# Two small masks of the linear mixers on ScalarE and GpSimd instead of VectorE, and twelve matmuls without a reader

## The chip, the cores and the metric

The kernel runs on one core of a Trainium2 chip. The engines of a core each work through a queue of their own, in order: PE (TensorE, matmuls), DVE (VectorE), ACT (ScalarE), POOL (GpSimd) and SP (which here issues the loads of weights). An instruction waits at the head of its queue until the semaphores say that what it reads is written and what it overwrites has been read. The metric is the device time of one execution, in microseconds (us), as the median of several runs. Of PE the profile also gives the granted clock: 1.00 is 2.4 GHz, 0.50 is 1.2 GHz.

## The reference

For 256 tokens of width 1024 a network of four layers is computed, all in fp32. Two layers of the first kind come first, f0 and f1:

```python
for l in range(DEPTH):                       # DEPTH = 2
    h = rms_norm(x, pre_mix_g[l])
    z = h @ w_in[l]                          # split into the inputs of four mixers
    o_a = hgrn2_mixer(a_q, a_f, a_i, a_g, ...)       # chunk_gla, 64 wide keys
    o_b = gla_mixer(b_q, b_k, b_v, b_code, b_g, ...) # chunk_gla, 32 wide keys
    o_c = mla_mixer(...)                             # softmax attention
    o_d = gdn_mixer(...)                             # gated delta rule
    mix = jnp.concatenate([o_a, o_b, o_c, o_d], axis=-1) @ w_out[l]
    x = x + rms_norm(mix, post_mix_g[l])
    h = rms_norm(x, pre_ffn_g[l])
    y = conv_glu_ffn(h, w_gate[l], w_up[l], conv_w[l], w_down[l])
    x = x + rms_norm(y, post_ffn_g[l])
```

Mixers a and b, which the change is about, share one form. Within a chunk of 64 tokens it is

```python
diff = b_[:, :, :, None, :] - b_[:, :, None, :, :]     # b_: running sum of log gates, per key channel
decay = jnp.where(causal, jnp.exp(jnp.where(causal, diff, 0.0)), 0.0)
attn = jnp.einsum('bhid,bhjd,bhijd->bhij', q_, k_, decay)
o = einsum(attn, v_) + einsum(q_ * exp(b_), state)
```

so each entry of `attn` needs a decay of its own for each channel, and only entries with j <= i count. Two layers of a second kind (s0, s1: four softmax attentions, a wide FFN, a gated embedding) follow.

## The kernel before

**Matmuls.** The weights come in fp32 by DMAs that SP issues, into tiles `raw`. ACT copies `raw` to a rounded high half `wh` (L300), and DVE, for some units POOL, subtracts to get the low half `wl` (L303). A product is three matmuls, high by high, high by low, low by high (`mm3`, L329 to L331). The tokens are two tiles of 128, t = 0 and 1; in the projections that close a layer, `acc` are the PSUM banks of tile 0 and `pc` those of tile 1.

**A layer of the first kind.** `norms` with `steps` (L454 to L514) makes the normed input: squares summed by ACT (L428) and DVE (L437), a power on POOL (L241), the product `nxn` on DVE (L502), eight transposes on PE (L505), and the halves by ACT (L510) and DVE (L512). The stretch from the last matmuls of one part through these steps to the first matmuls of the next I call a boundary; here its kind is 'in' where it leads into f1, '2in' where it leads into s0 or s1. Then the four mixers run in phases, in the order d, b, a, c with their first and second parts interleaved. I call the stretch with d's preparation and the body of b stage 1 (82 to 98 us in f0, 466 to 496 us in f1), and the one with the body of a, the attention of c and the end of d stage 2 (130 to 199 us, 515 to 592 us). Stage 2 ends in the output projection, `big_out`, whose units are taken in the order d, c, a, b.

**The body of a and b, `gla` (L691).** `A[t]`, 128 tokens by 4 heads by 128 tokens, collects `attn`, transposed, for tile t. For the diagonal, PE multiplies k by q (L704) and DVE multiplies the result by the identity (L705), which also zeroes the rest of `A[t]`. The rest goes level by level: at level s each block of 2s tokens gives its lower left square of s by s, in which the decays can be split at the middle of the block, so that one exponential each for rows and columns is enough. Gates are differenced on DVE and POOL (L721 to L728), exponentiated on ACT (L729), multiplied into q by DVE (`gl_r`, L733) and into k by POOL (`gl_e`, L737); PE multiplies (L743, L751). Level 128 goes to its own tile X, level 64 is copied by ACT (L756), levels 32, 16, 8, 4, 2 and 1 by DVE with a mask (L760), two instructions each. Then PE multiplies `A[t]` and X by v (L768, L769), and `head_norm` (L597) closes: square on ACT (L601), sum on DVE (L603), power on POOL (L236, L241), two products on DVE (`hn_y` L606, `hn_o` L608), transposes on PE (L415), halves `mT` by ACT (L417) and DVE (L418). The gla bodies of both mixers write the PSUM banks `pa`, two buffers in turn; `gla` is called four times.

**What sets the order.** Within mixers a scheduler that simulates a timeline orders each engine's queue as the program is built. At the boundaries the orders of PE or DVE are written out by hand. `warm` (L444) issues matmuls that nobody reads; `WARM` says how many for which tile.

Of the kernel before, what the change touches and what calls it, by code (L numbers as in the profile page):

```python
# [16 lines left out]
AF = mybir.ActivationFunctionType  # L17
OP = mybir.AluOpType
# [15 lines left out]
PEORD = ('in', '2in')  # L34
# [9 lines left out]
ASPL = 1  # L44
NEAR = 6
GATE = {"in": (3, 6), "ffn": (3, 4), "2in": (3, 4), "2ffn": (3, 4), "ple": (3, 4), "end": (3, 4)}
WARM = ((0, 0, 0), (0, 2, 0))

def steps_in_order(text):
    return [("AB".index(o[0]), int(o[1:])) for o in text.split()]  # L50
# [89 lines left out]
class K:  # L140
# [282 lines left out]
    def sum_sq(self, a, b, psum=False):  # L423

        nc = self.nc
        ssq = self.s(2, "ssq")
        sc = self.z([128, 512], "nsc", dt=BF)
        nc.scalar.activation(sc, a, AF.Square, scale=1.0 / 32, accum_out=ssq[:, 0:1])  # L428
        self.warm(sc, WARM[self.g == "a"][0 if psum else 2])
        yield  # L430
        if psum:
            sc = self.z([128, 512], "nsc", dt=BF)
            nc.scalar.activation(sc, b, AF.Square, scale=1.0 / 32, accum_out=ssq[:, 1:2])
            self.warm(sc, WARM[self.g == "a"][1])
        else:
            sc = self.z([128, 512], "nsc")
            nc.vector.scalar_tensor_tensor(sc, b, 1.0 / D, b, op0=OP.mult, op1=OP.mult, accum_out=ssq[:, 1:2])  # L437
        yield
        m = self.s(1, "msq")
        nc.vector.tensor_scalar(m, ssq[:, 1:2], ssq[:, 0:1], EPS, op0=OP.add, op1=OP.add)  # L440
        self.r = self.pow(m, 1)
        yield
# [248 lines left out]
    def gla(self, nft, b, qm, k, v, finish, g):  # L691

        nc = self.nc
        n = nft * 256
        ft = [0, 1] if nft == 2 else [0, 0]
        A = [self.z([128, 4, 128], "gl_a") for _ in range(2)]
        for t in range(2):  # L700
            ts = slice(t * 128, t * 128 + 128)
            p = self.pt().rearrange("p (h i) -> p h i", h=4)
            for j in range(2):
                nc.tensor.matmul(p[:, 2 * j:2 * j + 2], k[:, ft[j], ts], qm[j][:, :, ts], start=True, stop=True)  # L704
            nc.vector.tensor_tensor(A[t], p, self.ident[:, None, :].to_broadcast([128, 4, 128]), OP.mult)  # L705
            yield
        b4 = b.rearrange("p f (c s) -> p f c s", s=64)
        last = [b4[:, :, c, 63:64].to_broadcast([128, nft, 64]) for c in range(4)]
        for lv, s in enumerate((128, 64) + LEVELS):
            E = self.z([128, nft, 256], "gl_e", g)  # L710
            ev = E.rearrange("p f (b two s) -> p f b two s", two=2, s=s)
            e4 = E.rearrange("p f (c s) -> p f c s", s=64)
            if s == 128:
                nc.vector.tensor_tensor(e4[:, :, 1], last[1], b4[:, :, 1], OP.subtract)
                nc.vector.tensor_tensor(e4[:, :, 0], last[0], b4[:, :, 0], OP.subtract)
                nc.vector.tensor_tensor(e4[:, :, 0], e4[:, :, 0], last[1], OP.add)
                nc.gpsimd.tensor_copy(e4[:, :, 2], b4[:, :, 2])
                nc.vector.tensor_tensor(e4[:, :, 3], b4[:, :, 3], last[2], OP.add)
            elif s == 64:
                for c in (0, 2):  # L720
                    nc.vector.tensor_tensor(e4[:, :, c], last[c], b4[:, :, c], OP.subtract)  # L721
                    nc.gpsimd.tensor_copy(e4[:, :, c + 1], b4[:, :, c + 1])
            else:
                bv = b.rearrange("p f (b two s) -> p (f b) two s", two=2, s=s)
                ee = E.rearrange("p f (b two s) -> p (f b) two s", two=2, s=s)
                ref = bv[:, :, 0, s - 1:s].to_broadcast([128, n // (2 * s), s])
                nc.vector.tensor_tensor(ee[:, :, 1], bv[:, :, 1], ref, OP.subtract)
                nc.gpsimd.tensor_tensor(ee[:, :, 0], ref, bv[:, :, 0], OP.subtract)  # L728
            nc.scalar.activation(E, E, AF.Exp)  # L729
            R = self.z([128, 2, 2, 128], "gl_r", g)  # L730
            for j in range(2):
                qv = qm[j].rearrange("p h (b two s) -> p h b two s", two=2, s=s)[:, :, :, 1]
                nc.vector.tensor_tensor(R[:, j].rearrange("p h (b s) -> p h b s", s=s),  # L733
                                        ev[:, ft[j], :, 1][:, None].to_broadcast([128, 2, 128 // s, s]), qv, OP.mult)
            kv = k.rearrange("p f (b two s) -> p (f b) two s", two=2, s=s)
            kk = E.rearrange("p f (b two s) -> p (f b) two s", two=2, s=s)
            nc.gpsimd.tensor_tensor(kk[:, :, 0], kk[:, :, 0], kv[:, :, 0], OP.mult)  # L737
            yield
            p = self.pt()
            if s == 128:  # L740
                p = p.rearrange("p (j h i) -> p j h i", j=2, h=2)
                for j in range(2):
                    nc.tensor.matmul(p[:, j], E[:, ft[j], :128], R[:, j], start=True, stop=True)  # L743
                X = self.z([128, 4, 128], "gl_x")
                nc.scalar.activation(X, p.rearrange("p j h i -> p (j h) i"), AF.Copy)
                continue
            M = 64 if s == 64 else 128
            p = p[:M].rearrange("p (t j h i) -> p t j h i", t=2, j=2, h=2)
            for t in range(2):
                for j in range(2):  # L750
                    nc.tensor.matmul(p[:, t, j], E[:, ft[j], t * 128:t * 128 + M], R[:, j, :, t * 64:t * 64 + 64],  # L751
                                     start=True, stop=True)
            for t in range(2):
                pv = p[:, t].rearrange("p j h i -> p (j h) i")
                if s == 64:
                    nc.scalar.activation(A[t][:64, :, 64:128], pv, AF.Copy)  # L756
                    continue
                nb = 64 // s
                mask = self.cu[:, (lv - 2) * 64:(lv - 1) * 64].rearrange("p (b s) -> p b s", s=s)
                nc.vector.copy_predicated(A[t].rearrange("p h (b two s) -> p h b two s", two=2, s=s)[:, :, :, 1],  # L760
                                          mask[:, None].to_broadcast([128, 4, nb, s]),
                                          pv.rearrange("p h (b s) -> p h b s", s=s))
        yield
        for t in range(2):
            o = self.pt()[:, :256].rearrange("p (h d) -> p h d", h=4)
            for h in range(4):
                if t:
                    nc.tensor.matmul(o[:, h], X[:, h], v(0)[:, h * 64:h * 64 + 64], start=True, stop=False)  # L768
                nc.tensor.matmul(o[:, h], A[t][:, h], v(t)[:, h * 64:h * 64 + 64], start=not t, stop=True)  # L769
            finish(t, o)  # L770
            yield
# [1016 lines left out]
```

## Time and profile before

| what | value |
|---|---|
| median of 3 runs | 1531.16 us (1528.4 to 1532.23) |
| the profiled execution | 1537.6 us |
| its span, first to last instruction | 1535.9 us |
| mean granted clock of PE | 0.989 |
| PE busy | 1481.3 us, 96% |
| DVE busy | 1062.3 us, 69% |
| ACT busy | 837.2 us, 55% |
| POOL busy | 281.8 us, 18% |

Busy shares are averages over stages with different limits: DVE with 69% over the span is busy without a break in some stretches of the mixers. So what one engine's instruction is worth has to be read from the stage that it stands in. A busy PE at clock 0.50 takes twice as long for the same matmul.

### The profile page before, as it was taken

To read this page: it belongs to the slowest core of one execution; us is meant where nothing else is said; L and a number is where in the kernel's file an instruction comes from. 1 tells how busy PE (TensorE), PEld (TensorE's weight loads), DVE (VectorE), ACT (ScalarE), POOL (GpSimd) and SP (SyncE) were. 2 spreads that over 40 slices of the span, in tenths; PEclk is the share of its full clock that TensorE was granted. 3 is DMA by queue.
4 is the path that set the end of the run, shared out by engine and by line. 5 is a ranking of instruction groups with operands and counts; after the bars stand their busy time and mean duration, and the time that the engine had idled before them with its cause. 6 is when DMAs were issued, how large, how long until landed. Compare 5 with 4: busy or idle time off the path is not lost.

```text
span 1535.9 us, 23550 instructions
## 1 busy us (share of the span) xinstructions
PE 1481.3 (96%) x8731; PEld 1287.0 (84%) x8739; DVE 1062.3 (69%) x1891; ACT 837.2 (55%) x1520; POOL 281.8 (18%) x375
## 2 busy tenths in 40 slices
PE   7999999999998999999999999999998999999998
PEld 7988888888897987888978887888877888888886
DVE  6897577667789756777766866566657695666655
ACT  5735456556574534655545665544554675544453
POOL 1544210000254322000042122000024231100010
PEclk9999999999999999999999999999999999999999
DMA  7422146666452214666646334566653533465663
GB/s 238 150 84 100 52 140 184 190 190 213 135 161 78 93 42 134 183 192 187 206 131 184 110 112 124 187 191 191 211 186 111 163 121 108 133 192 187 190 202 108
DMA packets 156418, 233.99 MB, mean 152 GB/s; under 512 B 11700, under 2 KB 118158, under 8 KB 156302
## 3 DMA queue, kind: packets, MB, share of 16 engines
q1 hardware_dynamic: 156302, 232.48, 49.0%
q8 instruction: 69, 1.13, 0.3%
q14 instruction: 47, 0.39, 0.1%
HBM read 231.40 MB, written 1.05 MB: 151 GB/s over the span
## 4 chain that ended last, share of the span: by engine, by line
PE 79%; DVE 10%; ACT 4%; POOL 2%; DMA 2%; issue 2%; SPq 0%; ACTq 0%; DVEq 0%; POOLq 0%
PE pa L375 8%; PE pd L375 7%; PE acc L329 7%; PE acc L331 7%; PE acc L330 7%; PE pc L329 5%; PE pc L331 5%; PE pc L330 5%; PE pd L376 4%; PE pa L376 4%; PE pa L329 2%; PE pa L331 2%; PE pa L330 2%; DVE wl L303 2%; DVE gl_r L733 1%
## 5 line engine op out<-in xcount | busy, mean ns | idle before, releaser
L303 DVE TENSOR_TENSOR wl<-raw,wh 128x1024 fp32r<-128x1024 f32 (+4 forms) x424 | 487.1, 1157 | 310.2 <-ACT wh L300 308.6
L300 ACT ACTIVATE wh<-raw 128x1024 fp32r<-128x1024 f32 (+4 forms) x420 | 433.1, 1035 | 368.9 <-PE pc L331 92.1
L303 POOL TENSOR_TENSOR wl<-raw,wh 128x1024 fp32r<-128x1024 f32 (+1 forms) x26 | 61.2, 2358 | 641.8 <-ACT wh L300 611.2
L375 PE MATMUL pa<-xT,wh 128*128 128x512 f32 x392 | 145.9, 397 | 0.0
L375 PE MATMUL pd<-xT,wh 128*128 128x512 f32 x392 | 145.7, 397 | 0.0
L376 PE MATMUL pd<-xT,wl 128*128 128x256 f32 x392 | 110.2, 281 | 0.3 <-DVE wl L303 0.3
L376 PE MATMUL pa<-xT,wl 128*128 128x256 f32 x392 | 110.1, 281 | 0.0
L375 PEld LDWEIGHTS pd<-xT,wh 128*128 128x128 f32 x392 | 73.6, 188 | 16.8
L375 PEld LDWEIGHTS pa<-xT,wh 128*128 128x128 f32 x392 | 73.7, 188 | 12.3
L330 PE MATMUL acc<-wl,f_h 128*128 128x512 f32 x200 | 78.0, 390 | 0.0
L330 PE MATMUL pc<-wl,f_h 128*128 128x512 f32 x200 | 77.8, 389 | 0.0
L331 PE MATMUL pc<-wh,f_l 128*128 128x512 f32 x200 | 77.5, 389 | 0.0
L331 PE MATMUL acc<-wh,f_l 128*128 128x512 f32 x200 | 77.3, 391 | 0.0
L376 PEld LDWEIGHTS pd<-xT,wl 128*128 128x128 f32 x392 | 74.0, 189 | 3.6 <-DVE wl L303 0.5
L376 PEld LDWEIGHTS pa<-xT,wl 128*128 128x128 f32 x392 | 74.1, 189 | 3.6
L330 PE MATMUL acc<-wl,xT 128*128 128x512 f32 (+4 forms) x200 | 71.1, 357 | 1.6 <-DVE wl L303 1.6
L329 PE MATMUL acc<-wh,xT 128*128 128x512 f32 (+4 forms) x200 | 71.5, 361 | 1.2 <-ACT xT L510 0.8
L329 PE MATMUL pc<-wh,f_h 128*128 128x512 f32 x200 | 71.4, 390 | 0.0
L331 PE MATMUL acc<-wh,xT 128*128 128x512 f32 (+4 forms) x200 | 70.4, 354 | 0.6 <-DVE xT L512 0.6
L329 PE MATMUL acc<-wh,f_h 128*128 128x512 f32 x200 | 67.0, 391 | 0.0
L329 PE MATMUL acc<-wh,mT 128*128 128x512 f32 (+2 forms) x136 | 51.4, 387 | 1.6 <-ACT mT L510 1.4
L330 PE MATMUL acc<-wl,mT 128*128 128x512 f32 (+2 forms) x136 | 51.3, 378 | 0.0
(651 smaller groups left out, 3852.5 us busy)
## 6 DMA issues: line engine op xcount, KB each, us to landing
raw<-in_w_in_dram SPq DMA_DIRECT2D x84, 512.0 KB, 4.2
raw<-in_w_mlp_up_dram SPq DMA_DIRECT2D x64, 512.0 KB, 3.7
raw<-in_w_mlp_down_dram SPq DMA_DIRECT2D x64, 512.0 KB, 3.6
raw<-in_ffn_w_gate_dram SPq DMA_DIRECT2D x44, 512.0 KB, 3.6
raw<-in_ffn_w_up_dram SPq DMA_DIRECT2D x44, 512.0 KB, 3.9
raw<-in_ffn_w_down_dram SPq DMA_DIRECT2D x44, 512.0 KB, 3.6
raw<-in_w_out_dram SPq DMA_DIRECT2D x32, 512.0 KB, 3.6
raw<-in_w_ple_gate_dram SPq DMA_DIRECT2D x16, 512.0 KB, 4.4
```

The costliest lines, as they stand in the source:

```text
L300: nc.scalar.activation(h[:, p], raw[:, p], AF.Copy)
L303: e.tensor_tensor(l[:, p], raw[:, p], h[:, p].bitcast(F), OP.subtract)
L329: t.matmul(out, ah, bh, start=first, stop=False, skip_group_check=True)
L330: t.matmul(out, ah, bl, start=False, stop=False, skip_group_check=True)
L331: t.matmul(out, al, bh, start=False, stop=last, skip_group_check=True)
L375: t.matmul(out[f], h[:, k, c], xT.both[:, :, kk], start=kk == 0, stop=False, skip_group_check=True)
L376: t.matmul(out[f][:, 1], l[:, k, c], xT[0][:, kk], start=False, stop=kk == 7, skip_group_check=True)
L733: nc.vector.tensor_tensor(R[:, j].rearrange("p h (b s) -> p h b s", s=s), ev[:, ft[j], :, 1][:, None].to_broadcast([128, 2, 128 // s, s]), ...
```

## The change

Three edits. (1) At the boundaries of kinds 'in' and '2in', tile 0's sum of squares before the mixers (`sum_sq` without PSUM) is followed by four matmuls of the identity by the square `nsc`, 512 columns each, that nobody reads. There are three such boundaries: f0 to f1 (at 391 us), f1 to s0 (784) and s0 to s1 (1157). (2) The diagonal of `A[t]`: instead of the product with the identity on DVE, ACT copies the PSUM bank to `A[t]`, and POOL sets to zero what lies on one side of the diagonal; the levels overwrite the entries on the other side. (3) Level 32 is copied by ACT, four copies of 32 rows in each call of `gla`, two for each tile, without a mask.

```diff
--- before.py
+++ after.py
@@ -44,7 +44,7 @@
 ASPL = 1
 NEAR = 6
 GATE = {"in": (3, 6), "ffn": (3, 4), "2in": (3, 4), "2ffn": (3, 4), "ple": (3, 4), "end": (3, 4)}
-WARM = ((0, 0, 0), (0, 2, 0))
+WARM = ((0, 0, 0, 4), (0, 2, 0, 0))
 
 def steps_in_order(text):
     return [("AB".index(o[0]), int(o[1:])) for o in text.split()]
@@ -426,7 +426,7 @@
         ssq = self.s(2, "ssq")
         sc = self.z([128, 512], "nsc", dt=BF)
         nc.scalar.activation(sc, a, AF.Square, scale=1.0 / 32, accum_out=ssq[:, 0:1])
-        self.warm(sc, WARM[self.g == "a"][0 if psum else 2])
+        self.warm(sc, WARM[self.g == "a"][0 if psum else 2 + (self.near > 0 and self.kinds[self.near] in PEORD)])
         yield
         if psum:
             sc = self.z([128, 512], "nsc", dt=BF)
@@ -702,7 +702,10 @@
             p = self.pt().rearrange("p (h i) -> p h i", h=4)
             for j in range(2):
                 nc.tensor.matmul(p[:, 2 * j:2 * j + 2], k[:, ft[j], ts], qm[j][:, :, ts], start=True, stop=True)
-            nc.vector.tensor_tensor(A[t], p, self.ident[:, None, :].to_broadcast([128, 4, 128]), OP.mult)
+
+            nc.scalar.activation(A[t], p, AF.Copy)
+            nc.gpsimd.affine_select(out=A[t], in_=A[t], pattern=[[0, 4], [1, 128]], compare_op=OP.is_ge, fill=0.0,
+                                    base=0, channel_multiplier=-1)
             yield
         b4 = b.rearrange("p f (c s) -> p f c s", s=64)
         last = [b4[:, :, c, 63:64].to_broadcast([128, nft, 64]) for c in range(4)]
@@ -754,6 +757,10 @@
                 pv = p[:, t].rearrange("p j h i -> p (j h) i")
                 if s == 64:
                     nc.scalar.activation(A[t][:64, :, 64:128], pv, AF.Copy)
+                    continue
+                if s == 32:
+                    for r in (0, 64):
+                        nc.scalar.activation(A[t][r:r + 32, :, r + 32:r + 64], pv[r:r + 32, :, r // 2:r // 2 + 32], AF.Copy)
                     continue
                 nb = 64 // s
                 mask = self.cu[:, (lv - 2) * 64:(lv - 1) * 64].rearrange("p (b s) -> p b s", s=s)
```

In the linear mixers of both layers the schedule is laid out anew by the scheduler, with the same result in f0 and f1 in stage 2. Three places follow, in the rows of the engines' queues; line numbers after the change are higher by 3 behind the new lines of the diagonal and by 7 behind those of level 32.

PE at the end of stage 2 in f0 (f1 has the same rows), before: from the last matmul of d's tile 1 (L1240; sm_p and sm_pt belong to c's attention, hn_o to the head norms) to the first of the output projection of tile 1:

```order
L415 MATMUL pc<-cf,hn_o 128x128 x2
L655 MATMUL pc<-cf,sm_p 128x128 x4
L329 MATMUL acc<-wh,mT 128x512
L330 MATMUL acc<-wl,mT 128x512
L329 MATMUL acc<-wh,mT 128x512
L330 MATMUL acc<-wl,mT 128x512
L666 MATMUL pc<-c_v,sm_pt 128x64 x8
L331 MATMUL acc<-wh,mT 128x512 x2
L415 MATMUL pa<-cf,hn_o 128x128 x2
L415 MATMUL pd<-cf,hn_o 128x128 x2
L415 MATMUL pc<-cf,hn_o 128x128 x2
L329 MATMUL pc<-wh,mT 128x512
```

and after, where L1240 has become L1247:

```order
L1247 MATMUL pd<-d_vn,d_AT 128x64
L330 MATMUL acc<-wl,mT 128x512
L331 MATMUL acc<-wh,mT 128x512
L415 MATMUL pc<-cf,hn_o 128x128 x2
L415 MATMUL pd<-cf,hn_o 128x128 x2
L329 MATMUL pc<-wh,mT 128x512
L330 MATMUL pc<-wl,mT 128x512
```

The transposes of sm_p, the products with sm_pt, four of the six `acc` matmuls and two of the four pairs of hn_o transposes have been moved ahead of d's last matmul.

DVE in stage 1 of f1, before, around the second product with the identity:

```order
L1129 TENSOR_TENSOR d_AT<-pd,d_L 128x2x128
L733 TENSOR_TENSOR gl_r<-gl_e,gl_q 128x256 x2
L721 TENSOR_TENSOR gl_e<-a_b 128x2x64 x2
L705 TENSOR_TENSOR gl_a<-pa,cf 128x512
L733 TENSOR_TENSOR gl_r<-gl_e,gl_q 128x256 x2
L1155 COPY_PREDICATED d_V<-cu,d_MT 128x256
L1128 TENSOR_TENSOR d_MT<-pd,d_L 128x2x128
L1129 TENSOR_TENSOR d_AT<-pd,d_L 128x2x128
```

and the same place after:

```order
L1136 TENSOR_TENSOR d_AT<-pd,d_L 128x2x128
L736 TENSOR_TENSOR gl_r<-gl_e,gl_q 128x256 x2
L724 TENSOR_TENSOR gl_e<-a_b 128x2x64 x2
L736 TENSOR_TENSOR gl_r<-gl_e,gl_q 128x256 x2
L1162 COPY_PREDICATED d_V<-cu,d_MT 128x256
L1135 TENSOR_TENSOR d_MT<-pd,d_L 128x2x128
L1136 TENSOR_TENSOR d_AT<-pd,d_L 128x2x128
```

L705 is gone, and the rows around it keep their order.

PE at the boundary s0 to s1 after the change, from the last matmul of s0 to the first of s1; before, the same rows stand there without the eight of L449:

```order
L331 MATMUL pc<-wh,xT 128x512
L449 LDWEIGHTS cb
L449 MATMUL pa<-nsc,cb 128x512
L449 LDWEIGHTS cb
L449 MATMUL pa<-nsc,cb 128x512
L449 LDWEIGHTS cb
L449 MATMUL pa<-nsc,cb 128x512
L449 LDWEIGHTS cb
L449 MATMUL pa<-nsc,cb 128x512
L505 MATMUL pd<-cf,nxn 128x128 x8
L329 MATMUL acc<-wh,mT 128x512
```

The four matmuls wait for ACT's square, and L505 now stands behind them.

## Rows read from the trace of the kernel before

**Rows 1.** The page: busy times, and the chain that ended last.

```profile
PE 1481.3 (96%) x8731; PEld 1287.0 (84%) x8739; DVE 1062.3 (69%) x1891; ACT 837.2 (55%) x1520; POOL 281.8 (18%) x375
...
PE 79%; DVE 10%; ACT 4%; POOL 2%; DMA 2%; issue 2%; SPq 0%; ACTq 0%; DVEq 0%; POOLq 0%
```

**Rows 2.** Windows, stage 1: length, PE, PEld, DVE, ACT, POOL busy, clock, DMA, GB/s.

```profile
94.00:97.90 3.90, 2.21 (x14) 1.47 (x13) 3.90 (x10) 0.60 (x1) 1.58 (x5) 1.00 0.13 51
484.00:490.70 6.70, 4.09 (x29) 3.38 (x29) 6.70 (x15) 2.00 (x5) 4.50 (x8) 0.98 0.00 0
```

**Rows 3.** Windows of half clock, same columns.

```profile
97.90:104.35 6.45, 6.45 (x31) 6.00 (x30) 5.18 (x15) 1.48 (x4) 2.76 (x6) 0.50 0.01 3
490.70:497.10 6.40, 6.35 (x30) 6.06 (x30) 4.89 (x16) 0.42 (x1) 1.10 (x2) 0.50 0.20 61
551.90:558.70 6.80, 6.80 (x24) 5.60 (x25) 2.87 (x12) 3.23 (x15) 2.03 (x5) 0.50 0.00 0
1159.30:1166.10 6.80, 6.10 (x18) 4.99 (x19) 5.13 (x10) 2.64 (x5) 2.27 (x1) 0.51 0.00 0
```

**Rows 4.** Lines of the code: duration ns min/median/max, first and last start, forms.

```profile
L705 DVE TENSOR_TENSOR gl_a<-pa,cf x8: 676/678/683, 88.4 to 524.5; 128x512 f32<-128x512 f32 x8
...
L760 DVE COPY_PREDICATED gl_a<-cu,pa x48: 415/432/780, 103.9 to 550.3; 128x256 f32<-128x256 uint8 x48
...
L1068 POOL TENSOR_SCALAR_AFFINE_SELECT d_L<-d_L x4: 637/642/650, 53.9 to 438.1; 128x512 f32<-128x512 f32 x4
...
L1187 ACT ACTIVATE d_V<-pd x12: 250/268/379, 141.6 to 539.8; 32x128 f32<-32x128 f32 x8, 64x256 f32<-64x256 f32 x4
```

**Rows 5.** Timeline of DVE, stage 1 of f1: start us, us, instructions, count.

```profile
479.46 0.68 DVE L705 TENSOR_TENSOR gl_a<-pa,cf 128x512 f32<-128x512 f32 x1
480.06 0.74 DVE L733 TENSOR_TENSOR gl_r<-gl_e,gl_q 128x256 f32<-128x256 f32 x2
...
483.13 3.46 DVE L733 TENSOR_TENSOR gl_r<-gl_e,gl_q 128x256 f32<-128x256 f32 x6
...
489.01 0.76 DVE L760 COPY_PREDICATED gl_a<-cu,pa 128x256 f32<-128x256 uint8 x2
```

**Rows 6.** Timeline of POOL, stage 1 of f1.

```profile
484.11 0.91 POOL L737 TENSOR_TENSOR gl_e<-gl_e,a_k 128x256 f32<-128x256 f32 x1
```

**Rows 7.** Window in stage 2 of f0, columns as before.

```profile
145.00:163.00 18.00, 16.90 (x142) 14.38 (x140) 17.55 (x41) 10.05 (x24) 9.08 (x13) 1.00 0.35 118
```

**Rows 8.** Timeline of PE, end of stage 2, f0; [idle time before].

```profile
176.47 0.39 PE L1240 MATMUL pd<-d_vn,d_AT 128*128 128x64 f32 x2
...
181.10 0.38 PE L415 MATMUL pd<-cf,hn_o 128*128 128x128 f32 x2
...
182.01 0.50 PE L329 MATMUL pc<-wh,mT 128*128 128x512 f32 x1 [0.31 <-ACT mT L417]
```

**Rows 9.** Timelines of POOL, DVE and ACT, same place.

```profile
178.10 1.01 POOL L241 TENSOR_TENSOR rs<-rq_m,mhalf 128x4 f32<-128x4 f32 x1
...
179.82 0.43 DVE L608 TENSOR_TENSOR hn_o<-hn_y,a_g 128x256 f32<-128x256 f32 x1
...
181.58 0.38 ACT L417 ACTIVATE mT<-pd 128x256 fp32r<-128x256 f32 x1
```

**Rows 10.** Timeline of PE at the three boundaries into mixers.

```profile
391.59 0.39 PE L331 MATMUL pc<-wh,f_l 128*128 128x512 f32 x1
391.83 1.03 PE L505 MATMUL pd<-cf,nxn 128*128 128x128 f32 x8
...
786.71 1.64 PE L505 MATMUL pd<-cf,nxn 128*128 128x128 f32 x8 [3.10 <-DVE nxn L502]
...
1160.00 1.94 PE L505 MATMUL pd<-cf,nxn 128*128 128x128 f32 x8 [3.54 <-DVE nxn L502]
...
1169.44 1.03 PE L505 MATMUL pa<-cf,nxn 128*128 128x128 f32 x8
```

**Rows 11.** Timeline of DVE at the boundary s0 to s1.

```profile
1167.00 1.42 DVE L502 SCALAR_TENSOR_TENSOR nxn<-x,rs,gain 128x512 f32<-128x512 f32 x2 [2.51 <-POOL rs L241]
```

## The prediction

> **What bounds the kernel now.** I read the totals first. TensorE (PE) is busy for 96% of the span and carries 79% of the chain that ended last; DVE follows with 10% of that chain [rows 1]. So an edit on DVE, ACT or POOL pays only where PE stands still or runs slowly for want of them. I looked for such stretches with the table of windows. There are two kinds.
>
> The first is stage 1 of the linear mixers, the end of d's preparation with the body of mixer b (82 to 98 us in layer f0, 466 to 496 in f1). There the roles are reversed: DVE is busy for the whole of 94.00 to 97.90 and of 484.00 to 490.70, while PE works 2.21 of 3.90 and 4.09 of 6.70 us [rows 2]. What is taken off DVE there shortens the stage one for one, as long as DVE stays the last.
>
> The second kind is half clock. In four stretches of 6.4 to 6.8 us the granted clock is 0.50, which is 1.2 GHz, although PE is busy throughout them; three lie in the mixers, one at the boundary s0 to s1 [rows 3]. Each costs about half its length, 3.2 to 3.4 us, against full clock. Each comes behind a place where PE had gaps. The execution shown took 1537.6 us, 1.7 more than its span and 6.4 more than the median of 1531.2; I sum against its span and carry the difference over to the median unchanged.
>
> **Diagonal and level 32 in stage 1.** The DVE product with the identity goes eight times, 0.68 us each [rows 4]. In the queue it takes 0.60, from 479.46 to the next start at 480.06 [rows 5]. Two of them stand in the busy DVE stretch of each layer: 2 x 0.60 = 1.2 us. The level-32 pair, 0.76 us at 489.01 [rows 5], stands in it too in f1. In f0 it comes at 103.9 us [rows 4], inside a half-clock stretch in which PE works 6.45 of 6.45 us [rows 3], so it frees nothing there. Gross: -1.2 in f0 and -1.95 in f1, together -3.15.
>
> The replacements run elsewhere. Each ACT copy of a 32-row block takes about 0.27 us by its likes [rows 4], four in a row 1.1 us, and the copy of 128x512 less than the whole of that. ACT is busy 0.60 of 3.90 and 2.00 of 6.70 us there [rows 2], so this is hidden; if ACT were late, the DVE pair of level 16 and PE's use of the next PSUM bank would wait up to 1.1 us, beside the 0.76 saved. The POOL select has a twin, the affine_select at L1068, 0.64 us [rows 4]. It is read by nobody soon, but it is not free for DVE. Six DVE products gl_r took 3.46 us from 483.13, while two of them take 0.74 where POOL reads nothing [rows 5], which by a step of 0.33 makes six 2.1; in the longer stretch POOL was running its own products, one of 0.91 us at 484.11 [rows 6]. So DVE lost 1.4 us to POOL. Four selects of 0.64 in the two stage-1 stretches can therefore hand back between 0 and 2.6 us. I take half, 1.3, because about half of DVE's instructions there have both inputs in SBUF. Net for stage 1: -1.9, between -3.15 and -0.6. ("Who interferes with whom" on the page "SBUF — State Buffer" of the Trainium skill says that a DVE instruction with two SBUF inputs and a GpSimd instruction that reads SBUF block one another for a whole instruction; the rows agree in kind, and the rule taken at its worst would set the net at the upper bound.)
>
> **The same edits in stage 2** (mixer a with the attention of c and the end of d; 130 to 199 us, 515 to 592). Here PE is bound. It idles 1.10 us of 145 to 163 in f0 [rows 7]. With two DVE products and a pair less per gla, and the level-32 bank given back by ACT, I let all of that 1.1 go in each layer; the bounds are 0 and 1.1.
>
> But the schedule was laid out anew, and it moves work of c ahead. Before, between the last L1240 of tile 1 of d and the first `L329 pc<-wh,mT` of the output projection stood some 5 us of other work: transposes and products of c and `acc` matmuls. That covered the head norm of d's tile 1. The rows of order show that only two `acc` matmuls and four transposes are left there. The chain itself: L1240 ends at 176.47 + 0.39 = 176.86 [rows 8]; the power on POOL runs 178.10 to 179.11, the gated product hn_o on DVE ends at 180.25, and ACT's copy of 0.38 us precedes L329 [rows 9]. In the trace L415 pd began only at 181.10, and L329 at 182.01 after 0.31 us of idleness [rows 8]. If L415 starts as soon as hn_o is there, the chain comes down from 182.01 - 176.86 = 5.15 to about 4.3 us. The work left beside it is 2 matmuls at 0.23 and two pairs of transposes at 0.22, 0.9 us. PE would idle 4.3 - 0.9 = 3.4 instead of 0.3: +3.1 a layer. The lower bound is 0, if PE reaches that place late anyway; the upper is +3.1 with no gain upstream. Taken: 3.1 - 1.1 = +2.0 a layer, +4.0 for both.
>
> **The warm matmuls** stand between the last `L331 pc` and the transposes L505 at the three boundaries into mixers. At f0 to f1, L505 follows L331 at once (391.59, then 391.83, a step of 0.24) with no idleness, and the clock is full: L505 takes 1.03 us [rows 10]. Four matmuls of 512 columns at that step delay everything behind by +0.9 (between 0 and 0.96). At f1 to s0 PE idles 3.10 us before L505, which then takes 1.64 us [rows 10], 0.6 more than at full clock; at s0 to s1 it idles 3.54 and takes 1.94. The four run inside those gaps, since the square that they read is ACT's and comes long before nxn, so they cost nothing, and they leave shorter gaps. If the clock then stays full, s0 to s1 has up to 3.4 us to gain [rows 3]; but the transposes of tile 1, at 1169.44 [rows 10], cannot come before their nxn, whose two halves DVE begins at 1167.00 [rows 11], the first done some 0.6 later, so I count 1169.44 - 1167.6 = 1.8. At f1 to s0 I count 0.4 of the 0.6 that L505 loses, for tile 1 waits for DVE there as well. Sum: 0.9 - 0.4 - 1.8 = -1.3, between +0.9 (the clock falls all the same) and -4.0. (The Trainium skill, "TensorE: Matmul & The Clock Gate", Part 1, says that activity releases the throttle and idleness sets it; the trace agrees where half clock follows the two gaps. No row here shows whether four matmuls suffice.)
>
> **Clock in the mixers.** The stretch from 490.70 follows PE's gaps in 484.00 to 490.70; with DVE ahead and level 32 off it, those get shorter, and I count half of that one stretch, -1.6 (bounds 0 and the three mixer stretches, -9.8).
>
> **Sum.** -1.9 + 4.0 - 1.3 - 1.6 = -0.8. The execution would span 1535.1, and the median come to 1530.4 us.
>
> **Rivals.**
> - *The clock holds.* Denser PE keeps it full in two or all of the mixer stretches: -6.5 to -9.8 in place of -1.6, which gives 1525.5 to 1522; with the boundary at its best, 1520. For it: the gaps are just what the edits shorten. Against it: in 94.00 to 97.90 PE works only 57% of the time, and 0.6 us less DVE work leaves it sparse.
> - *The tail of stage 2 stalls and the clock falls.* The mechanism is the 3.4 us gap before `L329 pc` in f0 and f1. At the boundaries gaps of 3.10 and 3.54 us were followed by half clock, the latter for 6.8 us [rows 3, 10]. If that follows here, it costs up to 3.4 us a layer; I take 2.5, so +5.0. With the stage-1 stretch kept (+1.6) the time is 1530.4 + 6.6 = 1537, slower than before. It decides from the point where that gap is as long as those two. For it: the order. Against it: PE may reach the place late enough that the chain is partly done.
> - *Little comes of it.* POOL's selects block DVE for their whole length, warm matmuls only cost. Stage 1 gives -0.6, the boundaries +0.9, the clock nothing, stage 2 half of its loss, +2.0: 1531.2 + 2.3 = 1533.5.
>
> **How the numbers follow.** The forecast has 0.42, with its own range 1526 to 1534; the clock that holds 0.27; the falling clock in the tail 0.19; little 0.12. A measurement of this kernel can tell about 0.3%, 4.6 us, so faster means under 1526.6 and slower over 1535.8. Faster: 0.9 of the second case and a fifth of the first, 0.33. Slower: 0.8 of the third and a fifth of the fourth, with a little of the first, 0.20. Same: 0.47. The range 1520.5 to 1537.5 leaves out the far ends of the clock cases.
>
> **What the profile of the changed kernel will show.** Stage 1 of f1 should end about 1 to 2 us sooner, with DVE still at its limit and no DVE instruction of line 705; a gl_r product beside a select that takes over 0.9 us would confirm the blocking. In the tail of stage 2 the row of the first `L329 pc<-wh,mT` should have an idle time of about 3 us on ACT's mT, in both layers, and the clock row behind it tells the second rival. At s0 to s1, L505 should take about 1.0 us instead of 1.94. I am wrong if that idle time is under 1 us, if the half-clock stretches of the mixers vanish as a group, or if DVE's work in stage 1 does not shrink.

## The result and the profile after

The changed kernel takes 1542.38 us (median of 6 runs, 1536.36 to 1545.45) against 1533.35 for the kernel before in the same comparison: ratio 1.0063, interval 1.0043 to 1.0084, slower by 9.0 us by the medians and by 9.7 by the ratio. The forecast was 1530.4 with a range up to 1537.5. The second rival, the stall in the tail of stage 2 with a falling clock, was put at 1537 and is nearest, but it has neither the whole size nor, as the runs show, the whole place.

The page of the changed kernel, busy times and shares of the chain, to hold against [rows 1]:

```profile
span 1542.3 us, 23598 instructions
...
PE 1480.3 (96%) x8742; PEld 1283.2 (83%) x8751; DVE 1054.8 (68%) x1875; ACT 846.7 (55%) x1544; POOL 288.6 (19%) x383
...
PE 76%; DVE 10%; ACT 5%; DMA 4%; POOL 3%; issue 2%; SPq 0%; ACTq 0%; DVEq 0%; POOLq 0%
```

PE does the same work (and twelve matmuls more) in a span that is 6.4 us longer. Its share of the chain falls from 79 to 76% and those of ACT, DMA and POOL rise: PE waits more. The same PE instructions, found in both traces, say where. Times are starts in us, the last column is the difference that arose since the line above.

| PE instruction | before | after | since the line above |
|---|---|---|---|
| f0, stage 1: first L704 of b | 82.04 | 81.82 | -0.2 |
| f0, stage 2: first L704 of a | 130.20 | 127.96 | -2.0 |
| f0: first `L329 pc<-wh,mT` | 182.01 | 188.14 | +8.4 |
| f0: first matmul of the next boundary | 201.04 | 209.33 | +2.2 |
| f0 to f1: L505 | 391.83 | 401.78 | +1.7 |
| f1, stage 2: first L704 of a | 518.62 | 525.12 | -3.4 |
| f1: first `L329 pc<-wh,mT` | 573.57 | 581.75 | +1.7 |
| f1: first matmul of the next boundary | 592.62 | 602.11 | +1.3 |
| s0 to s1: L505 | 1160.00 | 1168.07 | -1.4 |
| behind s0 to s1: L505 of tile 1 | 1169.44 | 1175.98 | -1.5 |

Stage 1 came out shorter, stage 2 lost over 10 us in f0. The f1 rows are milder only because of the clock: the trace before had a half-clock stretch of 6.8 us in stage 2 of f1 [rows 3] and the one after has such a stretch in f0, from 166 us, and a shorter one at 582 us. With 3.4 us for each long stretch (half its length) taken out, stage 2 up to the first `L329 pc<-wh,mT` is 5.0 us longer in f0 and 5.1 in f1. The waits of PE are alike in both layers. Here is f0, with the idle time before each row in brackets; the last two answer to [rows 8]:

```profile
148.20 1.13 PE L754 MATMUL pa<-gl_r,gl_e 128*128 128x128 f32 x8 [1.34 <-DVE gl_a L767]
...
160.88 1.10 PE L776 MATMUL pa<-a_v,gl_a 128*128 128x64 f32 x8 [0.80 <-DVE gl_a L767]
...
164.86 0.44 PE L415 MATMUL pd<-cf,hn_o 128*128 128x128 f32 x2 [1.46 <-DVE hn_o L608]
...
187.01 0.66 PE L415 MATMUL pd<-cf,hn_o 128*128 128x128 f32 x2 [2.56 <-DVE hn_o L608]
188.14 0.79 PE L329 MATMUL pc<-wh,mT 128*128 128x512 f32 x1 [0.47 <-ACT mT L417]
```

Together with 0.3 to 0.5 us of smaller ones these are about 7.0 us of PE waiting in stage 2 of a layer. Before it was 1.5: the 0.31 of [rows 8] and, in f0,

```profile
160.76 0.27 PE L672 MATMUL pc<-cb 128*128 128x256 bf16 x1 [0.36 <-ACT sm_p L634]
...
162.15 1.10 PE L769 MATMUL pa<-a_v,gl_a 128*128 128x64 f32 x8 [0.68 <-DVE gl_a L760]
163.44 0.44 PE L415 MATMUL pd<-cf,hn_o 128*128 128x128 f32 x2 [0.18 <-DVE hn_o L608]
```

Two layers make 11 us more, of which stage 1 gave some back. Behind the waits the clock falls. Windows after the change with the columns of [rows 2]: stage 1's window of f0, two of half clock in f0, one in f1:

```profile
94.00:97.90 3.90, 2.50 (x15) 1.75 (x15) 3.90 (x9) 0.60 (x1) 2.62 (x6) 1.00 0.01 2
166.00:173.00 7.00, 7.00 (x32) 6.39 (x32) 1.78 (x6) 1.55 (x5) 0.58 (x2) 0.51 0.00 0
186.50:193.50 7.00, 6.02 (x15) 4.52 (x16) 2.01 (x3) 1.44 (x2) 0.00 (x0) 0.51 0.01 2
490.00:497.50 7.50, 7.04 (x33) 6.62 (x34) 6.26 (x16) 2.05 (x6) 3.91 (x7) 0.54 0.00 0
```

The first wait, 1.34 us, goes with level 32 on ACT: with that edit alone it is 1.20 us, with the diagonal alone 0.28. L754 waits for a PSUM bank that DVE's pair of level 16 gives back. The rows of ACT, POOL and DVE ahead of it:

```profile
142.54 1.09 ACT L763 ACTIVATE gl_a<-pa 32x128 f32<-32x128 f32 x4
143.65 1.12 ACT L1194 ACTIVATE d_V<-pd 32x128 f32<-32x128 f32 x4
...
145.19 0.63 ACT L732 ACTIVATE gl_e<-gl_e 128x512 f32<-128x512 f32 x1
...
146.06 0.92 POOL L740 TENSOR_TENSOR gl_e<-gl_e,a_k 128x256 f32<-128x256 f32 x1
...
145.86 1.41 DVE L736 TENSOR_TENSOR gl_r<-gl_e,gl_q 128x256 f32<-128x256 f32 x2 [0.28 <-ACT gl_e L732]
147.29 0.76 DVE L767 COPY_PREDICATED gl_a<-cu,pa 128x256 f32<-128x256 uint8 x2
```

ACT runs four copies of level 32 (L763) and four of d (L1194), then one of c's v, and only at 145.19 the exponential, whose input DVE had ready at 145.10. DVE's two gl_r then take 1.41 us instead of 0.74 [rows 5] beside POOL's product, and the pair ends at 148.05. The wait of 1.46 us is another kind. PE began the products L1217 of d's tile 0 at 30.2 us into stage 2, where it had been 26.2, and ACT squares them later still. Before, the square stood 0.4 us behind their end; now it is 2.1. The first two rows are from before, the others from after:

```profile
156.35 1.00 PE L1210 MATMUL pd<-d_vn,d_AT 128*128 128x64 f32 x8
...
157.72 0.37 ACT L601 ACTIVATE hn_sq<-pd 128x256 f32<-128x256 f32 x1
...
158.16 1.00 PE L1217 MATMUL pd<-d_vn,d_AT 128*128 128x64 f32 x8
...
160.31 0.47 ACT L634 ACTIVATE sm_p<-pc,sm_nb 128x256 f32<-128x256 f32 x1 [1.00 <-DVE sm_nb L629]
...
161.23 0.38 ACT L601 ACTIVATE hn_sq<-pd 128x256 f32<-128x256 f32 x1
...
160.06 0.20 DVE L629 TENSOR_SCALAR sm_nb<-sm_mx 128x2 f32<-128x2 f32 x1
...
164.41 0.40 DVE L608 TENSOR_TENSOR hn_o<-hn_y,a_g 128x256 f32<-128x256 f32 x1
```

The square (L601, 161.23) stands in ACT's queue behind exponentials of c, which waited for DVE's 160.06, and d's transposes L415 come last. Measured from the first L704 of stage 2, d's last matmul starts at 46.4 us before and at 55.5 after in f0 (3.4 of it half clock); work of c has gone ahead of d.

Stage 1 shows the price of POOL's selects. One stands beside DVE's subtraction in f1; another, in f0, beside gl_r:

```profile
483.79 1.35 POOL L707 TENSOR_SCALAR_AFFINE_SELECT gl_a<-gl_a 128x512 f32<-128x512 f32 x1 [1.17 <-ACT gl_a L706]
...
483.63 1.01 DVE L303 TENSOR_TENSOR wl<-raw,wh 128x832 fp32r<-128x832 f32 x1
...
94.31 0.82 POOL L707 TENSOR_SCALAR_AFFINE_SELECT gl_a<-gl_a 128x512 f32<-128x512 f32 x1
...
94.56 0.85 DVE L736 TENSOR_TENSOR gl_r<-gl_e,gl_q 128x256 f32<-128x256 f32 x1
```

Beside the subtraction only POOL paid: the select took 1.35 us instead of 0.64, while the subtraction took 1.01 us, as it does elsewhere in this trace (1.01 at 88.54). Beside gl_r both paid: the select took 0.82 us, and the gl_r 0.85 instead of the 0.41 of an undisturbed one. That an instruction of DVE with two SBUF inputs contends with one of POOL that reads SBUF is what the page "SBUF — State Buffer" of the Trainium skill ("Who interferes with whom") says; both rows agree. Three of the four selects of stage 1 stand beside such a gl_r, some 1.3 us in all, which is the price that the prediction took. DVE is still busy for all of 94.00 to 97.90.

At s0 to s1 the gap before L505 fell from 3.54 us [rows 10] to

```profile
1165.92 1.04 PE L449 MATMUL pa<-nsc,cb 128*128 128x512 bf16 x3
1168.07 1.32 PE L505 MATMUL pd<-cf,nxn 128*128 128x128 f32 x8 [1.11 <-DVE nxn L502]
```

and there is no half clock behind it.

### The profile page after: what moved, and what is told of

It reads as the page before. It is cut to its first block, busy times and chain, and to the rows that moved or that the text cites. A ratio compares the mean times of both kernels' runs of the same rounds, so it can differ in the third digit from the quotient of the medians.

```text
span 1542.3 us, 23598 instructions
## 1 busy us (share of the span) xinstructions
PE 1480.3 (96%) x8742; PEld 1283.2 (83%) x8751; DVE 1054.8 (68%) x1875; ACT 846.7 (55%) x1544; POOL 288.6 (19%) x383
## 4 chain that ended last, share of the span: by engine, by line
PE 76%; DVE 10%; ACT 5%; DMA 4%; POOL 3%; issue 2%; SPq 0%; ACTq 0%; DVEq 0%; POOLq 0%
PE pa L375 7%; PE pd L375 7%; PE acc L331 6%; PE acc L329 6%; PE acc L330 6%; PE pc L329 5%; PE pc L331 5%; PE pc L330 5%; PE pd L376 4%; PE pa L376 4%; PE pa L329 2%; PE pa L331 2%; PE pa L330 2%; DVE wl L303 2%; ACT wh L300 2%
## 5 line engine op out<-in xcount | busy, mean ns | idle before, releaser
L329 PE MATMUL pc<-wh,f_h 128*128 128x512 f32 x200 | 71.4, 390 | 0.0
L329 PE MATMUL acc<-wh,xT 128*128 128x512 f32 (+4 forms) x200 | 70.5, 356 | 1.0 <-ACT xT L510 0.8
L329 PE MATMUL acc<-wh,f_h 128*128 128x512 f32 x200 | 67.0, 391 | 0.0
L329 PE MATMUL acc<-wh,mT 128*128 128x512 f32 (+2 forms) x136 | 50.1, 377 | 1.2 <-ACT mT L510 1.1
L331 PE MATMUL acc<-wh,mT 128*128 128x512 f32 (+2 forms) x136 | 50.3, 374 | 0.6 <-DVE mT L512 0.6
```

The source lines that it names most:

```text
L329: t.matmul(out, ah, bh, start=first, stop=False, skip_group_check=True)
L331: t.matmul(out, al, bh, start=False, stop=last, skip_group_check=True)
```

## Experiments

All are compared with the kernel before, timed on the same chip (its median was 1532.1 to 1533.3 us in them); where a figure in us stands beside a ratio it is worked out from the ratio. First the three parts alone.

**Warm matmuls alone**

```diff
-WARM = ((0, 0, 0), (0, 2, 0))
+WARM = ((0, 0, 0, 4), (0, 2, 0, 0))
...
```

> The kernel before with the twelve matmuls alone; the mixers' queues stay as they were. In the changed kernel's trace the three boundaries into mixers together moved the end by about -1.4 us (f0 to f1 +1.3, f1 to s0 +0.4, s0 to s1 -3.1). If that ledger holds for the edit by itself: -1.4 us against the kernel before, with no half clock behind s0 to s1. If the gain at s0 to s1 came only from the phase in which the changed kernel arrived there: +0.9 to +1.5 us, with the half clock still there.

Measured 1.0002 (0.9990 to 1.0015), +0.2 us. Its trace holds a lesson on the ledger: nothing was changed in the mixers, but two of the half-clock stretches of the kernel before are not there.

```profile
97.90:104.35 6.45, 5.59 (x44) 4.97 (x44) 6.45 (x17) 1.64 (x5) 3.29 (x7) 1.00 0.01 3
490.70:497.10 6.40, 5.63 (x49) 5.39 (x49) 5.91 (x16) 0.38 (x1) 0.96 (x3) 1.00 0.33 104
```

So in the mixers they come and go between executions of the same queues. Without them stage 1, from the first L704 of b to that of a, takes 46.8 us in f0 and 51.0 in f1, where the kernel before took 48.2 and 53.3: they had cost 1.4 and 2.3 us, less than half of their length, and at full clock DVE is busy for nearly all of that time. From here on I compare the waits of PE, which repeat to 0.3 us, and the timed ratios.

**Twelve instead of four**

```diff
-WARM = ((0, 0, 0), (0, 2, 0))
+WARM = ((0, 0, 0, 12), (0, 2, 0, 0))
...
```

> The kernel before with twelve matmuls without a reader at each of the three boundaries into mixers, instead of the change's four. At f0 to f1 they stand in PE's way, 12 x 0.22 = 2.7 us; at the other two they fit into gaps of 3.1 and 3.5 us. If such matmuls keep the clock up there: 2.7 less 1.7 to 3.4 at each of two boundaries in the executions in which it would have fallen, -2 to +1 us against the kernel before. If the clock at these boundaries does not hang on them: +2.5 to +3 us.

Measured 1.0017 (1.0006 to 1.0028), +2.6 us: the price at f0 to f1, where eleven recorded ones took

```profile
392.01 2.76 PE L449 MATMUL pa<-nsc,cb 128*128 128x512 bf16 x11
394.61 1.04 PE L505 MATMUL pd<-cf,nxn 128*128 128x128 f32 x8
```

Over all traces of this study, the eight kernels with such matmuls at f1 to s0 and s0 to s1 show no half clock behind these two boundaries in 16 passes. The eight without show it in 7 of 16, behind gaps of 1.5 to 3.5 us, six times for 3.4 us and once for 6.8; by half of the length that is 1.7 or 3.4 us each. By these counts the matmuls do keep the clock up. They would gain 2 x 7/16 x 2 us on average, 1.7, and at f0 to f1 four of them cost 0.9; the timed runs cannot tell that from nothing. The twelve cost as much as if they gained nothing, but their interval, +0.9 to +4.3 us, does not quite exclude the 1.7.

**Mixer b alone (stage 1), and its two halves.** The edit of the change under a condition:

```diff
+            if nft == 1:
+                nc.scalar.activation(A[t], p, AF.Copy)
+                nc.gpsimd.affine_select(out=A[t], in_=A[t], ...)
+            else:
+                nc.vector.tensor_tensor(A[t], p, self.ident[...]..., OP.mult)
...
+                if s == 32 and nft == 1:
+                    for r in (0, 64):
+                        nc.scalar.activation(A[t][r:r + 32, :, r + 32:r + 64], ..., AF.Copy)
+                    continue
```

> Diagonal and level 32 on ScalarE and POOL in mixer b alone (stage 1). The ledger by stages says -2.0 us in f0 and -3.1 in f1: about -5 us against the kernel before if the gain of stage 1 is the edit's own and is kept up to the end; -2 us if it is only DVE's work without the clock; 0 if PE-bound stage 2 swallows it. Both theories on stage 2 (its order, or the load of the new instructions) expect stage 2 as before, since PE's queue there is the same as before.

Measured 0.9978 (0.9969 to 0.9987), -3.4 us: faster. Stage 2 waits as before, 1.5 us a layer. With the first condition alone, and with the second alone:

> Only the diagonal of mixer b (stage 1) on ScalarE and POOL. DVE loses two products of 0.60 us in each layer, 2.4 us. If the time of stage 1 follows DVE's work: -1.2 to -2.4 us against the kernel before, the smaller figure if POOL's selects block DVE for half their length. If it is the level 32 that gave the gain of mixer b's run (-3.4): 0.

> Only level 32 of mixer b (stage 1) on ScalarE. DVE loses a pair of 0.76 us in each layer. If the time follows DVE's work: -0.8 to -1.5 us. If the pair hid beside PE in f0 and was waited for in f1 alone: -0.8. With the diagonal's run it should add up to about -3.4.

Measured 0.9981 (0.9966 to 0.9995), -2.9, and 0.9995 (0.9982 to 1.0008), -0.8 us. They add up to the run with both. The interval of the diagonal (-5.2 to -0.8 us) holds the full 2.4 us of DVE's removed work and half of it alike, so these runs do not tell what POOL's blocking took. Traces with the clock alike tell more. In the version for use, further down, half clock begins 24.9 us into stage 1 of f1, before it was 25.0, each time for 6.8 us, and the stage takes 52.2 instead of 53.3 us. In f0, without half clock, it takes 46.1 in that version and in mixer b alone, and 46.6 and 46.8 in mixer a alone and the matmuls alone. That makes -1.1 and about -0.6, together some -1.7. What the timed -3.4 has beyond that would have to be the clock; no run here shows it by itself.

**Mixer a alone (stage 2)**, the same with `nft == 2`:

> Both edits in mixer a alone (stage 2). PE's queue at the end of stage 2 is the changed kernel's. Both theories expect the loss here: +10 to +13.5 us against the kernel before (ledger: +8.4 and +2.2 in f0, +1.7 and +1.3 in f1), with a wait of about 2.6 us before the L415 of d's tile 1 in both layers. If the loss needs the arrival of stage 1 as well, it is under +5.

Measured 1.0077 (1.0063 to 1.0090), +11.8 us: the whole loss. PE waits 6.9 us in stage 2 of each layer. Each half alone:

> Only the diagonal of mixer a (stage 2) on ScalarE and POOL. PE's queue keeps its tail; some rows of stage 2 change places. Order theory: within 2 us of the kernel before. Load theory: about half of the loss of mixer a's two edits, +4 to +7 us.

> Only level 32 of mixer a (stage 2) on ScalarE. PE's queue keeps its tail and nearly all of its order. Order theory: within 2 us of the kernel before. Load theory: the other half of the loss, +4 to +7 us; the four ACT copies, 1.1 us, stand in ACT's queue ahead of d's copies in each layer.

Diagonal: 1.0029 (1.0018 to 1.0041), +4.5 us; level 32: 1.0001 (0.9988 to 1.0013), +0.2. PE's waits in stage 2 are 3.8 and 2.8 us a layer. Neither of them has the changed tail; the scheduler lays it out so only when both edits are in mixer a, and 4.5 + 0.2 is far from 11.8. The diagonal came out as the load theory had it, level 32 as the order theory had it; its 1.3 us more of waits a layer did not show in its time, so the waits are a guide and not the time itself. The two runs do not separate load from order either: of PE's 416 instructions in stage 2 of a layer, 384 keep the order before with level 32 alone, 323 with the diagonal alone and 285 in the changed kernel. The diagonal's own share shows as a wait for POOL, which does d's zeroes later:

```profile
150.76 0.68 PE L1189 MATMUL pd<-d_V,d_X 128*64 128x64 f32 x8 [1.27 <-POOL d_X L1170]
```

**One bond at the tail.** With `dlast` the last L1240 of d's tile 1, traced before c:

```diff
-            for h in range(4):
-                nc.tensor.transpose(p[:, h], P[h % 2][:, h // 2, kt * 128:kt * 128 + 128], self.ident)
+            with ExitStack() as stack:
+                if kt and self.dlast is not None:
+                    stack.enter_context(self.tc.issue_after(self.dlast))
+                for h in range(4):
+                    nc.tensor.transpose(p[:, h], P[h % 2][:, h // 2, kt * 128:kt * 128 + 128], self.ident)
...
```

> The changed kernel, with one bond of order: c's last four transposes of sm_p and the products behind them are issued on PE behind d's last matmul. Not an instruction is added or taken away, ACT, DVE and POOL have the same work. If the order of PE is what costs the time (theory one), the wait before d's last L415 falls from 2.6 us to under 1.2 in both layers and the half clock behind it goes or shrinks: -4 to -8 us against the changed kernel, so 0 to +5 against the kernel before. If the new instructions on ACT and POOL delay the chain whatever the order (theory two), the time stays within 1.5 us of the changed kernel.

Measured 1.0056 (1.0040 to 1.0071), +8.6 us, by the ratios 1 us better than the change. The wait of 2.56 is gone, but the cover brings waits of its own, for c's softmax copies and c's head norm on DVE:

```profile
183.02 1.77 PE L671 MATMUL pc<-c_v,sm_pt 128*128 128x64 f32 x14 [0.61 <-DVE sm_pt L663]
185.51 0.44 PE L415 MATMUL pc<-cf,hn_o 128*128 128x128 f32 x2 [0.71 <-DVE hn_o L994]
...
186.75 0.80 PE L329 MATMUL pc<-wh,mT 128*128 128x512 f32 x1 [0.47 <-ACT mT L417]
```

5.5 us of waits a layer are left. The gain is within what the load theory allowed, and the first form of the order theory, that the tail alone carries the loss, fell here.

**PE's whole order as before.** All of the change stays; PE's instructions in the mixers and output projection of f0 and f1 are bound in the order that they had before:

```diff
...
+        self.bind(n0, l)
...
+    def bind(self, n0, l):
+        pe = [i for i in self.nc.cur_bb.bb.instructions[n0:] if i.engine == mybir.EngineType.PE]
+        order = [pe[a + k] for a, n in PEBEFORE[l] for k in range(n)]
+        info = mybir.DependencyInfo(mybir.DependencyClass.NoSync, mybir.DependencyReason.DATA)
+        for a, b in zip(order, order[1:]):
+            self.tc.add_manual_dep(b, a.name, info, reason="bind")
```

> The changed kernel with PE's queue in the mixers and output projection of f0 and f1 tied to the order it had before the change (bonds of issue order alone); the new ACT and POOL instructions and the twelve matmuls stay, and ACT, DVE and POOL are ordered around PE by the scheduler. Order theory (the loss is PE's new order in stage 2, of which the first bond, at the tail, mended only a part): stage 2 as before, -9 to -13 us against the changed kernel, so -4 to 0 against the kernel before. Load theory (the new instructions on ACT's queue and POOL's reads delay DVE and the chain whatever PE's order): within 3 us of the changed kernel, +6 to +10 against the one before, with the 1.3 and 1.5 us waits still there.

Measured 1.0007 (0.9993 to 1.0021), +1.1 us: 8 to 9 of the change's 9.7 us are gone by an edit that adds no instruction and takes none away. That is outside both expectations, and near the order theory's. It is not PE's queue alone that went back, though, for the scheduler lays the other engines around it. Of ACT's 72 instructions in stage 2 of f0 before, 44 stand in the same order in the changed kernel and 68 in this run. So the run parts the layout of the queues from the load; whether PE's order or ACT's costs more it cannot say. What is left of waits in stage 2 of f0:

```profile
154.34 1.13 PE L755 MATMUL pa<-gl_r,gl_e 128*128 128x128 f32 x8 [0.77 <-DVE gl_a L768]
...
160.65 0.27 PE L673 MATMUL pc<-cb 128*128 128x256 bf16 x1 [1.14 <-ACT sm_p L635]
...
162.04 1.10 PE L777 MATMUL pa<-a_v,gl_a 128*128 128x64 f32 x8 [0.67 <-DVE gl_a L768]
...
181.89 0.51 PE L330 MATMUL pc<-wh,mT 128*128 128x512 f32 x1 [0.31 <-ACT mT L418]
```

3.2 us a layer, 1.7 more than before: that is the load of the new instructions on ACT and POOL, 3.4 us in two layers, about what stage 1 gains. Without the twelve matmuls:

> Diagonal and level 32 on ScalarE and POOL in both mixers, PE's queue in f0 and f1 tied to its order before the change, and no matmuls at the boundaries. The run with those matmuls gave +1.1 us against the kernel before. Order theory: stage 1 gains 3 us, stage 2 keeps waits of 1.7 us a layer more than before, so about 0 (-1 to +1); the matmuls' part is the difference to +1.1. Load theory: over +6.

Measured 1.0015 (1.0000 to 1.0030), +2.3 us: no difference from the run with them that these runs can tell.

**One half of the order each**

```diff
-        for a, b in zip(order, order[1:]):
-            self.tc.add_manual_dep(b, a.name, info, reason="bind")
+        for n in range(cut + 1, len(order)):          # cut: first product with kd, L1218
+            self.tc.add_manual_dep(order[n], order[n - 1].name, info, reason="bind")
```

> The changed kernel with PE's order tied to that before only from d's products with kd (L1218) on, in f0 and f1; the front of stage 2 as changed. Tail theory (the predicted wait of 3 us at the first L329 pc is the loss): that wait goes, -5.5 us and the half clock behind it, -5 to -9 against the changed kernel, 0 to +4 against the one before. Front theory (waits of 1.3, 0.8 and 1.5 us ahead of L1218, where c's prepared work stands before d's): 3.9 us a layer stay, +5 to +8 against the kernel before.

> The reverse: PE's order tied to that before up to L1218, and to the changed kernel's order behind it. Tail theory: the wait of 3 us stays, +6 to +9 us against the kernel before. Front theory: only 2.6 us a layer of waits ahead of L1218 are left, as in the run with the whole order tied, and the chain of d's tile 1 starts in time: +1 to +5 against the kernel before.

For the second, `PEBEFORE` was replaced by the order before up to `cut` and the changed one behind it. Measured 1.0046 (1.0031 to 1.0060), +7.1 us, with the tail as before; 1.0090 (1.0071 to 1.0108), +13.8 us, with the front as before. First the waits of the one, then those of the other:

```profile
149.46 1.13 PE L755 MATMUL pa<-gl_r,gl_e 128*128 128x128 f32 x8 [1.35 <-DVE gl_a L768]
...
161.84 1.10 PE L777 MATMUL pa<-a_v,gl_a 128*128 128x64 f32 x8 [0.80 <-DVE gl_a L768]
165.42 0.69 PE L416 MATMUL pd<-cf,hn_o 128*128 128x128 f32 x2 [2.48 <-DVE hn_o L609]
...
187.15 0.50 PE L330 MATMUL pc<-wh,mT 128*128 128x512 f32 x1 [0.31 <-ACT mT L418]
```

```profile
155.03 1.13 PE L755 MATMUL pa<-gl_r,gl_e 128*128 128x128 f32 x8 [0.77 <-DVE gl_a L768]
...
161.35 0.27 PE L673 MATMUL pc<-cb 128*128 128x256 bf16 x1 [1.15 <-ACT sm_p L635]
...
162.74 1.10 PE L777 MATMUL pa<-a_v,gl_a 128*128 128x64 f32 x8 [0.67 <-DVE gl_a L768]
...
189.60 0.66 PE L416 MATMUL pd<-cf,hn_o 128*128 128x128 f32 x2 [2.58 <-DVE hn_o L609]
190.74 0.79 PE L330 MATMUL pc<-wh,mT 128*128 128x512 f32 x1 [0.47 <-ACT mT L418]
```

Both halves cost, and the second more than either expectation allowed. The changed front alone leaves 5.3 us of waits a layer, the changed tail alone 6.0 and 6.7. The second kernel waits less than the change, and yet is slower; in its trace half clock lasts some 10 us in f0 ahead of the tail, in the change's some 7:

```profile
165.00:176.00 11.00, 10.96 (x48) 9.45 (x46) 3.45 (x10) 3.71 (x13) 2.05 (x5) 0.53 0.01 1
```

Whether that alone is the difference stays open, for such stretches vary.

**A version for use**: mixer b's two edits, and the matmuls at f1 to s0 and s0 to s1 only.

```diff
+        self.warm(sc, WARM[self.g == "a"][0 if psum else 2 + (self.near > 0 and self.kinds[self.near] == "2in")])
...
```

> The two edits in mixer b alone, and the matmuls without a reader at the boundaries f1 to s0 and s0 to s1 alone. Both theories expect the gain of the run with mixer b alone, -3 us, and some 1 to 3 us more from s0 to s1: -4 to -6 us against the kernel before. If the matmuls give nothing (as in their own run, +0.2), -3.

Measured 0.9980 (0.9967 to 0.9992), -3.1 us, the same as mixer b's edits alone. Both beat the kernel before and the changed one; the boundaries added nothing that can be seen.

## Why the prediction was wrong

**The step that failed** is "I let all of that 1.1 go in each layer", the gain upstream in stage 2. Its sign was wrong: ahead of d's L1218 PE waits 3.9 us a layer instead of 1.2. The reason given, less work on DVE, holds in stage 1, where DVE is the last. In stage 2 the last is the chain of d through PE, ACT, DVE and POOL, and the work was put on ACT and POOL, which that chain uses. I had counted ACT's room in stage 1 only [rows 2]. With PE's order as before, this load alone turns -1.1 into +1.7 a layer; the rest of the 2.7 us more comes with the new layout, which puts c's work ahead of d's in PE's queue and in ACT's.

**The tail** was right in kind and nearly in size: +3.1 us predicted, 2.56 + 0.47 - 0.31 = +2.7 measured in f0, 2.57 + 0.47 - 0.31 in f1. The comparison of the two orders had shown it. I read the order at the tail and not in the front, where c's work was moved ahead of d's as well. A sum by terms also missed that the two hang together: tied at the tail alone, the kernel kept most of the loss.

**The falling clock** of the second rival was there in f0, twice, at 166 and 186.5 us. In f1 a shorter stretch came at the tail. It belongs to the loss, but the size is not settled, since these stretches move between executions.

**Stage 1** was forecast at -1.9 and came to -2.0 and -3.4 us in the two layers of the traces, -5.4 in all. Much of that is the clock: in f0 the half-clock stretch is absent, and in f1 it stands elsewhere. Where the clock is alike, the two layers gain about 0.6 and 1.1 us, near the net 1.9, and the gl_r beside the selects show the 1.3 us that were set against the gross 3.15. The prediction's mark for the blocking, a gl_r of over 0.9 us beside a select, was met by one alone, of 0.93 us from 93.70 in f0, and that one stood mostly beside another product of POOL; the others took 0.85. The timed runs of mixer b say -3.4 (interval -4.7 to -2.0), close to the -1.9 and the -1.6 of the clock together, though no run shows the clock's part of it by itself.

**The boundaries**: f0 to f1 cost what was said, about 0.9, since the twelve cost 2.6. L505 at s0 to s1 took 1.32 us where about 1.0 was forecast and 1.94 stood. But the half clock there is not a fixed property of the kernel before: a sum of -1.3 from one profile was a sum from one draw. Timed, it is +0.2, between -1.5 and +2.3.

**The clock in the mixers** (-1.6) was of that kind too. The trace after has half clock from 490 us as well, but stage 1 of f1 begins 9.6 us later there: the stretch lies 15 us into the stage instead of 25. It is gone in the trace of the matmuls alone, which leave stage 1 as it was. Nor did these stretches cost half of their length: in stage 1 it was 1.4 us in f0 and 2.3 in f1, where 3.2 to 3.4 had been counted.

## What to carry to other kernels

Where a scheduler lays out the queues, an edit moves more than its instructions: compare the whole order of the bound engine in each stage that shifts, and ask what now stands ahead of the longest chain; bind the old order of one engine to separate the price of the layout from that of the load, and see how far the other queues followed. Take work off an engine only in the stage in which it is the last; the same edit in the next stage, put on engines that the longest chain runs through, cost over three times what it gave. One profile is one draw of the clock: before a half-clock stretch goes into a sum, see whether a run with the same queues has it.

## What had not been expected of the hardware

Half clock behind a gap is not certain: gaps of 1.5 to 3.5 us at two boundaries were followed by it in 7 of 16 passes, and stretches in the mixers with equal queues were there in one execution and absent in the next. In stage 1, where DVE is busy for nearly the whole of these stretches at full clock too, 6.8 us of half clock cost 1.4 and 2.3 us, not 3.4. A POOL select of 128x512 took 0.64 us in one place and 1.35 beside a subtraction of DVE, which itself took no longer than elsewhere; beside a select, a gl_r of DVE took 0.85 us instead of 0.41.
